# Decoder step on one core: memory tokens turned by VectorE in 32 x 32 blocks, with K/V weight rows loaded in the matching order

## The chip, the cores and the metric

The kernel runs on one core of a Trainium2 chip. The metric is the time of one execution on the device, in microseconds (us). Lower is better.

## The reference

One step of a decoder layer for 256 prompt tokens and 64 sample tokens (8 sequences of 8), 320 in all, with D = 2048, in float32. The parts that matter here:

```python
h = rms_norm(x, attn_norm_g);  z = h @ w_in       # u, v, glu_a, glu_b, q, gates
# three branches (spatial gating, conv module, cross-attention), gated, merged,
# @ w_o, then RMSNorm and a squared-ReLU MLP of 4*D, then a final RMSNorm
...
def mem_kv(mem, mem_norm_g, w_mem_kv):            # mem: 256 tokens x 2048
    kv = rms_norm(mem, mem_norm_g) @ w_mem_kv     # w_mem_kv: 2048 x 2048
    k, v = jnp.split(kv, 2, axis=-1)              # 1024 columns each, 4 heads of 256
```

K and V of the prompt's memory are outputs, and the prompt's cross-attention uses them.

## The kernel before, in words

All products run at float32 accuracy as three matmuls on two-part numbers: each operand is split into a high part (rounded to float32r) and a low part (the residue), and hi x hi, hi x lo and lo x hi are added in PSUM. ScalarE makes the high part of a weight tile (`split_to`, lines 252 and 278) and VectorE the low part (`residue_to`, recorded at line 44 as all VectorE work is).

The whole kernel is one list of 544 "halves". A half is 256 rows by 512 columns of some weight matrix, 512 KB, in two row blocks of 128 (k = 0, 1). Halves are grouped by 512 output columns; a group over 2048 rows has eight halves. In "T" halves the weights are the stationary operand and 320 tokens stream past (24 matmuls, lines 1341 to 1343). In "N" halves, those of `w_mem_kv`, the turned memory is stationary and 512 weight columns stream (twelve matmuls, lines 1371 to 1373). The order is: glu_b and glu_a (halves 0 to 31), q (32 to 47), kv (48 to 79, the N halves), the gate of branch C (80 to 111), u, v, and so on.

At the start of half i the loop asks for the weight load of half i+4 on SP's queue (`load_to`; three buffers `wraw`, so a load waits until VectorE is done with the one three before), then ScalarE's split of half i+2, then VectorE's residue of half i+1, and in the middle of the half VectorE's residue of half i+2. Everything else is a "side step", put by hand into the list `side[i]` of some half and issued between its matmuls (`spread` lays a list of steps over a range of halves, leaving out halves that end a group; `later` puts one step at one half).

The memory takes this way. `mem_load(0)` and `mem_load(1)` at halves 16 and 17 load 128 tokens per partition row (two token blocks by 1024 channels). Four `mem_sq_step`s in halves 22 to 31 add the squares of each token, which lie along one partition's row, on ScalarE. Sixteen `mem_tr_step`s in halves 32 to 47 turn one block of 128 channels each: two TensorE transposes into PSUM (line 748), then ScalarE's high part times the gain `mem_norm_g` (line 118), then VectorE's low part. `mh` and `ml` hold the turned memory, channel on the partition, token along the row; the root mean square of a token is multiplied in when K and V leave PSUM (`evac_kv`).

VectorE also computes the depthwise convolution, as 248 taps of two instructions each (`conv_step`), and these have no fixed place. `pace` adds taps to a half as long as the estimated VectorE time of the half (`V.spent`, by the rates of `PacedVector`: 0.08 us and 0.00105 us an element, a transpose 0.0023, copies 0.0006) stays under 0.75 of the half's 3.2 us (2.6 in N halves). Taps still left at half 184 are all issued there, ahead of the layer norm that needs them.

Of the kernel before, what the change touches and what calls it, by code (L numbers as in the profile page):

```python
# [10 lines left out]
F32R = mybir.dt.float32r  # L11
AF = mybir.ActivationFunctionType
ALU = mybir.AluOpType
AX = mybir.AxisListType

D = 2048
# [4 lines left out]
EPS = 1e-6  # L21
CONV_PACE = 0.75
WARM = 5
LO_HI, HI_LO, MEM_OFF = 40, 24, 8
QUARTER = (0, 1)


# [22 lines left out]
def decoder_step_kernel(  # L50
# [8 lines left out]
    nc = tc.nc  # L59
    V = PacedVector(nc.vector)  # L60
# [5 lines left out]
    def sb(shape, tag, dt=F32, bufs=1, name=None):  # L66
        counter[0] += 1
        return pool.tile(shape, dt, tag=tag, name=f"{name or tag}_{counter[0]}", bufs=bufs)
# [5 lines left out]
    def ps_misc(shape):  # L74
        counter[0] += 1
        return psum.tile(shape, F32, tag="misc", name=f"misc_{counter[0]}", bufs=2)
# [14 lines left out]
            for o in (0, 8 * NT + LO_HI)  # L91
        ]

    def mem_block(tag, name):
        flat = sb([128, 16 * 256 + MEM_OFF], tag, F32R, name=name)
        return flat[:, MEM_OFF:].rearrange("p (k t) -> p k t", t=256)

    def place():

# [10 lines left out]
    def f32(ap):  # L110
        return ap.bitcast(F32)
# [5 lines left out]
    def split_scaled(hi, lo, src, g):  # L117
        nc.scalar.activation(hi, src, AF.Copy, scale=g)
        V.scalar_tensor_tensor(
            out=lo, in0=src, scalar=g, in1=f32(hi), op0=ALU.mult, op1=ALU.subtract  # L120
        )
# [51 lines left out]
    def rstd_col(sums, scale, n=1, then=None, gap=1, between=()):  # L173
        c = sb([128, 3, 4], "rs", bufs=2)
        v, t, r = c[:, 0, :n], c[:, 1, :n], c[:, 2, :n]
        rstd_chain(v, r, lambda: t, sums, scale, then, gap, between)
        return r
# [48 lines left out]
    def pieces(j):  # L226
        return (slice(0, 1), slice(1, 2)) if j == 0 else (slice(0, 2),)

    def load_to(i):
        while issued[0] <= min(i, NH - 1):  # L230
            j = issued[0]
            g, h = halves[j]
            t = sb([128, 2, 512], "wraw", bufs=RAW_BUFS, name="wraw")
            r0 = (g["k0"] + 2 * h) * 128
            src = g["src"][r0:r0 + 256, g["n0"]:g["n0"] + 512].rearrange("(k p) n -> p k n", p=128)
            for ks in pieces(j):
                nc.sync.dma_start(t[:, ks], src[:, ks])
            raws[j] = t
            issued[0] += 1

# [21 lines left out]
    def split_alloc(j):  # L262
        hi = sb([128, 2, 512], "whi", F32R, bufs=3, name="whi")
        parts[j] = [hi, raws.pop(j)]

    def residue_alloc(j):
        parts[j].append(sb([128, 2, 512], "wlo", F32R, bufs=3, name="wlo"))
# [27 lines left out]
    def spread(lo, hi, steps):  # L295
        slots = [i for i in range(lo, hi) if not ends[i]] or [lo]
        for s, fn in enumerate(steps):
            side[slots[s * len(slots) // len(steps)]].append(fn)

    def later(at, fn):  # L300
        side[at].append(fn)

    S = {}


    def prologue():
        rest = sb([104, 128], "tr", bufs=3, name="vrows")
        S["rest"] = rest
        ag = sb([16, 128], "tr", bufs=3, name="agrows")
        nc.sync.dma_start(ag, attn_g[0].rearrange("(r c) -> r c", c=128))  # L310
        xn = sb([128, 2, D], "T1", name="xn")
        xs = sb([64, D], "T2", name="xs")
        xp_v = x_prompt[0].rearrange("(t p) d -> p t d", p=128)
        xs_v = x_sample.rearrange("b s d -> (b s) d")
        def x_load(c0, w):
            cs = slice(c0, c0 + w)
            nc.sync.dma_start(xn[:, :, cs], xp_v[:, :, cs])
            nc.sync.dma_start(xs[:, cs], xs_v[:, cs])

        S["x_load"] = x_load  # L320
        for j, (c0, w) in enumerate(((0, 256), (256, 256), (512, 512))):
            x_load(c0, w)
            load_to(j)

        S["ones"] = sb([128, 128], "ones")
        V.memset(S["ones"], 1.0 / 1024)
        wp = ps_misc([128, 512])
        for _ in range(WARM):
            nc.tensor.matmul(wp[:, :128], S["ones"], S["ones"], start=True, stop=True)
        warm = sb([128, 1], "warm")  # L330
        nc.scalar.activation(warm, S["ones"][:, 0:1], AF.Copy)
        S["xss"] = sb([128, 3, 4], "xss")
        V.memset(S["xss"], 1.0)
        ident = sb([128, 128], "ident")
        make_identity(nc, ident)
        S["ident"] = ident

        r0 = 0
        S["col"] = {"attn_g": 104}
        for name, src, n in (  # L340
            ("mlp_g", mlp_g, 16), ("mem_g", mem_g, 16), ("b_gate", b_gate, 48),
            ("conv_b", conv_b, 8), ("conv_ln_g", conv_ln_g, 8), ("conv_ln_b", conv_ln_b, 8),
        ):
            nc.gpsimd.dma_start(rest[r0:r0 + n, :], src[0].rearrange("(r c) -> r c", c=128))
            S["col"][name] = r0
            r0 += n
        vecs = sb([128, 120], "vecs")
        S["vecs"] = vecs
        vp = ps_misc([128, 512])
        nc.tensor.transpose(vp[:, :16], ag, ident[:16, :16])  # L350
        V.tensor_copy(vecs[:, 104:120], vp[:, :16])

        S["hh"] = sb([128, 16, NT], "HH", F32R, name="hh")
        S["hl"] = sb([128, 16, NT], "HL", F32R, name="hl")
        S["toks"] = [(xn[:, 0], 128, 0), (xn[:, 1], 128, 128), (xs, 64, 256)]
        split_alloc(0)
        residue_alloc(0)
        issued[1] = issued[2] = 1
        for k in range(2):
            x_in_step(k)  # L360
            split_part(0, k)
            residue_part(0, k)
        load_to(3)
        S["x_load"](1024, 512)

    def x_in_step(m):
        pt = ps_misc([128, 512])
        for a, p, c0 in S["toks"]:
            nc.tensor.transpose(  # L369
                pt[:, c0:c0 + p], a[:, 128 * m:128 * (m + 1)], S["ident"][:p, :p]  # L370
            )
        split(S["hh"][:, m], S["hl"][:, m], pt[:, :NT])
# [44 lines left out]
    def col(name, i):  # L417
        c = S["col"][name] + i
        return S["vecs"][:, c:c + 1]
# [293 lines left out]


    def mem_load(i):
        if i == 0:
            S["mem"] = [None, None]
            S["mss"] = sb([128, 2, 2], "mss")
        t = sb([128, 2, 1024], ("T7", "T4a")[i], name="mem")
        nc.sync.dma_start(  # L720
            t, mem_prompt[0, :, 1024 * i:1024 * (i + 1)].rearrange("(t p) d -> p t d", p=128)
        )
        S["mem"][i] = t

    def mem_sq_step(i, t):
        for c in range(2):
            d = sb([128, 512], "at", bufs=3)
            src = S["mem"][i][:, t, 512 * c:512 * (c + 1)]
            acc = sb([128, 1], "ss", bufs=3)
            nc.scalar.activation(d, src, AF.Square, accum_out=acc)  # L730
            tot = S["mss"][:, 0, t:t + 1]
            if i == 0 and c == 0:
                V.tensor_copy(tot, acc)
            else:
                V.tensor_tensor(out=tot, in0=tot, in1=acc, op=ALU.add)
        if i == 1 and t == 1:
            S["mrstd"] = sb([128, 2], "mrstd")
            r = rstd_col(
                S["mss"][:, 0], 1.0 / D, 2, lambda: V.tensor_copy(S["mrstd"], r)
            )  # L740

    def mem_tr_step(k):
        if k == 0:
            S["mh"] = mem_block("T1", "mh")
            S["ml"] = mem_block("T2", "ml")
        p = ps_misc([128, 2, 256])
        for t in range(2):
            nc.tensor.transpose(
                p[:, 0, 128 * t:128 * (t + 1)],
                S["mem"][k // 8][:, t, 128 * (k % 8):128 * (k % 8 + 1)], S["ident"],  # L750
            )
        split_scaled(S["mh"][:, k], S["ml"][:, k], p[:, 0], col("mem_g", k))

    def kT_step(n, t, kn):
        if n == 0 and t == 0:
# [460 lines left out]
    with tc.manual_schedule():  # L1216
# [17 lines left out]
        q0, kv0, u0, c0 = f[("q", 0)], f[("kv", 0)], f[("u", 0)], f[("gC", 0)]  # L1234
        v0, w0, a1, g0 = f[("v", 0)], f[("wC", 0)], f[("gA", 0)], f[("gB", 0)]
        later(16, lambda: mem_load(0))
        later(17, lambda: mem_load(1))
        spread(q0 - 10, q0, [lambda i=i, t=t: mem_sq_step(i, t) for i in range(2) for t in range(2)])
        spread(q0, q0 + 16, [lambda k=k: mem_tr_step(k) for k in range(16)])

        def attn_begin():
            hs = [attn_prompt_steps(h) for h in range(4)]
# [59 lines left out]
        for i, (g, h) in enumerate(halves):  # L1302
# [8 lines left out]
            hi, _, lo = parts.pop(i)  # L1311
            last = h == g["nk"] // 2 - 1
            if i == 0:
                for mi in range(4):
                    accs[mi] = ps_main([128, 512])
                for k in range(2):
                    for xs_, ws in ((0, hi), (1, hi), (0, lo)):
                        for mi in range(4):
# [3 lines left out]
                                stop=False,  # L1322
# [8 lines left out]
            elif g["kind"] == "T":  # L1331
                for mi in range(4):
                    if h == 0:
                        accs[mi] = ps_main([128, 512])
                    a = accs[mi][:, :NT]
                    c = 2 * (mi % 2) + mi // 2 if key[0] == "q" else mi
# [26 lines left out]
            else:  # L1363
                for t in range(2):
# [3 lines left out]
                    for k in range(2):  # L1368
                        kk = 2 * h + k
                        mh, ml = S["mh"][:, kk, ms], S["ml"][:, kk, ms]  # L1370
# [50 lines left out]
```

## Time and profile before

| what | value |
|---|---|
| time, median of 3 runs | 1978.63 us (1975.5 to 1981.38) |
| time of the profiled execution | 1981.95 us |
| its span in the profile | 1980.2 us |
| TensorE busy, share of the span | 1955.4 us, 99% |
| VectorE, ScalarE, GpSimd busy | 1184.9, 821.6 and 44.6 us |
| share of the chain that ended last: TensorE, DMA, VectorE | 94%, 2%, 2% |
| moved by DMA | 319.25 MB, 161 GB/s over the span |
| loads of `w_mem_kv`: count, size, median time from issue to landing | 32 of 512 KB, 4.1 us |
| loads of the memory | 2 of 1024 KB, 8.6 us |

How to read it: PE is TensorE's matmuls, PEld its weight loads, DVE is VectorE, ACT ScalarE, POOL GpSimd, SP the engine whose queue issues most loads. A line such as L748 is a line of the kernel. In a group's row stand the instruction, out<-in with the program's names, shapes, count, then busy time, mean nanoseconds of one, and the idle time before it with what ended it. Matmuls overlap, so their durations (0.3 us) are longer than the distance between two starts. In a table of stretches each row gives the stretch, its length, busy time and count for each engine, the granted TensorE clock, the busy share of the sixteen DMA engines, and GB/s.

### The profile page before, as it was taken

To read this page: it belongs to the slowest core of one execution; us is meant where nothing else is said; L and a number is where in the kernel's file an instruction comes from. 1 tells how busy PE (TensorE), PEld (TensorE's weight loads), DVE (VectorE), ACT (ScalarE), POOL (GpSimd) and SP (SyncE) were. 2 spreads that over 40 slices of the span, in tenths; PEclk is the share of its full clock that TensorE was granted. 3 is DMA by queue.
4 is the path that set the end of the run, shared out by engine and by line. 5 is a ranking of instruction groups with operands and counts; after the bars stand their busy time and mean duration, and the time that the engine had idled before them with its cause. 6 is when DMAs were issued, how large, how long until landed. Compare 5 with 4: busy or idle time off the path is not lost.

```text
span 1980.2 us, 32516 instructions
## 1 busy us (share of the span) xinstructions
PE 1955.4 (99%) x13316; PEld 1912.6 (97%) x13316; DVE 1184.9 (60%) x2079; ACT 821.6 (41%) x1185; POOL 44.6 (2%) x88
## 2 busy tenths in 40 slices
PE   9999999999999999999999999999999999999997
PEld 8999789898999999999999999999999999999997
DVE  4687786576788768655556554445434554455544
ACT  6465445445543445444444333333333333333333
POOL 0001000100100000000000000000000000000000
PEclk9999999999999999999999999999999999999998
DMA  6554864998644445454445445444445544455443
GB/s 213 184 150 150 211 220 110 228 206 217 185 157 144 149 140 160 139 167 153 149 160 171 147 141 170 150 150 145 154 160 152 151 143 162 153 156 146 149 155 107
DMA packets 189971, 319.25 MB, mean 161 GB/s; under 512 B 43761, under 2 KB 44489, under 8 KB 189686
## 3 DMA queue, kind: packets, MB, share of 16 engines
q1 hardware_dynamic: 184798, 302.56, 51.3%
q0 software_dynamic: 5024, 14.62, 2.9%
q8 instruction: 104, 1.70, 0.4%
q14 instruction: 45, 0.37, 0.1%
HBM read 311.48 MB, written 6.09 MB: 160 GB/s over the span
## 4 chain that ended last, share of the span: by engine, by line
PE 94%; DMA 2%; DVE 2%; ACT 1%; issue 0%; SPq 0%; DVEq 0%; ACTq 0%
PE acc L1341 29%; PE acc L1343 29%; PE acc L1342 29%; DMA wraw<-in_w_in_dram 2%; PE acc L1373 1%; PE acc L1372 1%; PE acc L1371 1%; DVE wlo L44 1%; DMA wraw<-in_w_mem_kv_dram 0%; PE misc L924 0%; PE misc L369 0%; PE misc L874 0%; PE acc L1319 0%; DVE dc L44 0%; PE misc L773 0%
## 5 line engine op out<-in xcount | busy, mean ns | idle before, releaser
L1341 PE MATMUL acc<-hh,whi 128*128 128x320 f32 x2424 | 756.2, 312 | 0.0
L1343 PE MATMUL acc<-hh,wlo 128*128 128x320 f32 x2424 | 748.7, 309 | 0.0
L1342 PE MATMUL acc<-hl,whi 128*128 128x320 f32 x2424 | 739.0, 305 | 0.0
L44 DVE TENSOR_TENSOR wlo<-wraw,whi 128x1024 fp32r<-128x1024 f32 x368 | 449.0, 1223 | 416.6 <-ACT whi L278 416.5
L278 ACT ACTIVATE whi<-wraw 128x1024 fp32r<-128x1024 f32 x368 | 389.5, 1058 | 690.6 <-PE acc L1342 571.8
L1341 PEld LDWEIGHTS acc<-hh,whi 128*128 128x128 f32 x2424 | 456.8, 188 | 8.4 <-issue 7.0
L1342 PEld LDWEIGHTS acc<-hl,whi 128*128 128x128 f32 x2424 | 456.6, 188 | 0.4
L1343 PEld LDWEIGHTS acc<-hh,wlo 128*128 128x128 f32 x2424 | 454.7, 188 | 0.0
L252 ACT ACTIVATE whi<-wraw,vecs 128x512 fp32r<-128x512 f32 x352 | 236.5, 720 | 278.2 <-PE acc L1342 184.2
L1341 PE MATMUL acc<-ah,whi 128*128 128x320 f32 x1024 | 315.8, 308 | 0.0
L1343 PE MATMUL acc<-ah,wlo 128*128 128x320 f32 x1024 | 315.5, 308 | 0.0
L1342 PE MATMUL acc<-al,whi 128*128 128x320 f32 x1024 | 311.4, 304 | 0.0
L44 DVE SCALAR_TENSOR_TENSOR wlo<-wraw,vecs,whi 128x512 fp32r<-128x512 f32 x352 | 248.6, 748 | 81.4 <-ACT whi L252 80.7
L1341 PEld LDWEIGHTS acc<-ah,whi 128*128 128x128 f32 x1024 | 192.5, 188 | 0.0
L1342 PEld LDWEIGHTS acc<-al,whi 128*128 128x128 f32 x1024 | 192.3, 188 | 0.0
L1343 PEld LDWEIGHTS acc<-ah,wlo 128*128 128x128 f32 x1024 | 191.5, 187 | 0.0
L44 DVE SCALAR_TENSOR_TENSOR dc<-cx,rstd,dc 128x256 f32<-128x256 f32 x480 | 153.2, 379 | 0.0
L1343 PE MATMUL acc<-moh,wlo 128*128 128x320 f32 x256 | 79.1, 309 | 0.0
L1341 PE MATMUL acc<-moh,whi 128*128 128x320 f32 x256 | 78.7, 308 | 0.0
L44 DVE TENSOR_TENSOR res<-res,acc 128x320 f32<-128x320 f32 x80 | 38.9, 486 | 66.5 <-PE acc L1343 66.4
L1342 PE MATMUL acc<-mol,whi 128*128 128x320 f32 x256 | 78.1, 305 | 0.0
L1072 ACT ACTIVATE ah<-tr 128x320 fp32r<-128x320 f32 x64 | 30.2, 472 | 66.9 <-DVE tr L44 66.9
(243 smaller groups left out, 1700.4 us busy)
## 6 DMA issues: line engine op xcount, KB each, us to landing
wraw<-in_w_in_dram SPq DMA_DIRECT2D x175, 512.0 KB, 4.4
wraw<-in_w_up_dram SPq DMA_DIRECT2D x128, 512.0 KB, 3.8
wraw<-in_w_down_dram SPq DMA_DIRECT2D x128, 512.0 KB, 3.7
wraw<-in_w_mem_kv_dram SPq DMA_DIRECT2D x32, 512.0 KB, 4.1
wraw<-in_w_o_dram SPq DMA_DIRECT2D x32, 512.0 KB, 3.7
cache<-in_cache_mem_k_dram SPq DMA_DIRECT2D x32, 256.0 KB, 7.7
cache<-in_cache_mem_v_dram POOLq DMA_DIRECT2D x32, 256.0 KB, 7.1
wraw<-in_w_c_out_dram SPq DMA_DIRECT2D x16, 512.0 KB, 4.0
```

The lines of the kernel that those rows point to most:

```text
L44: return fn(*args, **kw)
L252: nc.scalar.activation(hi, t, AF.Copy, scale=col("attn_g", 2 * h + k))
L278: nc.scalar.activation(parts[j][0], parts[j][1], AF.Copy)
L1072: nc.scalar.activation(out, in_, fn, **kw)
L1341: nc.tensor.matmul(a, hi[:, k, ms], xh, start=(kk == 0), stop=False)
L1342: nc.tensor.matmul(a, hi[:, k, ms], xl, start=False, stop=False)
L1343: nc.tensor.matmul(a, lo[:, k, ms], xh, start=False, stop=(last and k == 1))
L1371: nc.tensor.matmul(accs[t], mh, hi[:, k], start=(kk == 0), stop=False)
L1372: nc.tensor.matmul(accs[t], mh, lo[:, k], start=False, stop=False)
L1373: nc.tensor.matmul(accs[t], ml, hi[:, k], start=False, stop=(last and k == 1))
```

## The change

The memory is loaded in another layout. Tile i (of two) holds on partition 32q + r, at place g, 256 channels from 512q + 256i of token 32g + r. A 32 x 32 block transpose on VectorE, in place, then puts a channel on each partition and 256 tokens along the row, with no TensorE and no PSUM in it. Block k of the turned memory so holds channels 512q + 32k + j on partition 32q + j, where it held channels 128k + p. The rows of `w_mem_kv` are loaded in the same order: block k takes 32 rows from each quarter of the matrix, and each half's load is written as two loads of one block. The column of gains `mem_norm_g` is loaded in that order too. A token's squares now lie on four partitions, one for each quarter; one small matmul with a selection matrix (built from the identity) adds them over the quarters, and a mask picks the place of each token. The steps of halves 32 to 47 become one `mem_rstd_step` and sixteen `mem_turn_step`s.

```diff
@@ load_to
-            src = g["src"][r0:r0 + 256, g["n0"]:g["n0"] + 512].rearrange("(k p) n -> p k n", p=128)
-            for ks in pieces(j):
-                nc.sync.dma_start(t[:, ks], src[:, ks])
+            cols = slice(g["n0"], g["n0"] + 512)
+            if g["kind"] == "N":
+                src = g["src"][:, cols].rearrange("(q k i) n -> k q i n", q=4, i=32)
+                for k in range(2):
+                    nc.sync.dma_start(t[:, k], src[2 * h + k])
+            else:
+                src = g["src"][r0:r0 + 256, cols].rearrange("(k p) n -> p k n", p=128)
+                for ks in pieces(j):
+                    nc.sync.dma_start(t[:, ks], src[:, ks])
@@ prologue (rows of the small vectors)
-            nc.gpsimd.dma_start(rest[r0:r0 + n, :], src[0].rearrange("(r c) -> r c", c=128))
+            rows, dst = src[0].rearrange("(r c) -> r c", c=128), rest[r0:r0 + n, :]
+            if name == "mem_g":
+                rows = src[0].rearrange("(q k i) -> k q i", q=4, i=32)
+                dst = dst.rearrange("k (q i) -> k q i", i=32)
+            nc.gpsimd.dma_start(dst, rows)
@@ mem_load
-        t = sb([128, 2, 1024], ("T7", "T4a")[i], name="mem")
-        nc.sync.dma_start(
-            t, mem_prompt[0, :, 1024 * i:1024 * (i + 1)].rearrange("(t p) d -> p t d", p=128)
+        t = sb([128, 8, 256], ("T7", "T4a")[i], name="mem")
+        for q in range(4):
+            c0 = 512 * q + 256 * i
+            nc.sync.dma_start(
+                t[32 * q:32 * (q + 1)],
+                mem_prompt[0, :, c0:c0 + 256].rearrange("(g r) c -> r g c", r=32),
+            )
@@ squares: 16 of 256 channels in place of 8 of 512
+    def mem_sq_step(i, a):
+        for g in range(4 * a, 4 * a + 4):
+            d = sb([128, 512], "at", bufs=3)
+            nc.scalar.activation(
+                d[:, :256], S["mem"][i][:, g], AF.Square, accum_out=S["mss"][:, i, g:g + 1]
+            )
+    def mem_rstd_step():
+        mss, ident = S["mss"], S["ident"]
+        V.tensor_tensor(out=mss[:, 0], in0=mss[:, 0], in1=mss[:, 1], op=ALU.add)
+        sel = sb([128, 128], "at", bufs=3)
+        quarter = ident.rearrange("p (a r) -> p r a", a=4)
+        V.tensor_reduce(sel[:, 0:32], quarter, axis=AX.X, op=ALU.add)
+        for a in range(1, 4):
+            V.tensor_copy(sel[:, 32 * a:32 * (a + 1)], sel[:, 0:32])
+        p = ps_misc([128, 512])
+        nc.tensor.matmul(p[:, :8], sel, mss[:, 0], start=True, stop=True)
...
@@ turning
-        p = ps_misc([128, 2, 256])
-        for t in range(2):
-            nc.tensor.transpose(
-                p[:, 0, 128 * t:128 * (t + 1)],
-                S["mem"][k // 8][:, t, 128 * (k % 8):128 * (k % 8 + 1)], S["ident"],
-            )
-        split_scaled(S["mh"][:, k], S["ml"][:, k], p[:, 0], col("mem_g", k))
+        m = S["mem"][k // 8][:, :, 32 * (k % 8):32 * (k % 8 + 1)]
+        V.transpose(m, m)
+        hi, lo = (S[n][:, k].rearrange("p (g r) -> p g r", r=32) for n in ("mh", "ml"))
+        split_scaled(hi, lo, m, col("mem_g", k))
@@ order of steps
-        spread(q0, q0 + 16, [lambda k=k: mem_tr_step(k) for k in range(16)])
+        spread(q0, q0 + 16, [mem_rstd_step] + [lambda k=k: mem_turn_step(k) for k in range(16)])
```

The tiles `mh` and `ml` also start at new offsets inside their buffers (8 and 24 elements, where both had 8).

More of the change, by code (lines that the diff above doesn't have):

```diff
@@ L23 @@
 WARM = 5
-LO_HI, HI_LO, MEM_OFF = 40, 24, 8
+LO_HI, HI_LO = 40, 24
+MH_OFF, ML_OFF = 8, 24
 QUARTER = (0, 1)
@@ L92, in both, with mem_block @@
         ]
-    def mem_block(tag, name):
-        flat = sb([128, 16 * 256 + MEM_OFF], tag, F32R, name=name)
-        return flat[:, MEM_OFF:].rearrange("p (k t) -> p k t", t=256)
+    def mem_block(tag, name, off):
+        flat = sb([128, 16 * 256 + off], tag, F32R, name=name)
+        return flat[:, off:].rearrange("p (k t) -> p k t", t=256)
     def place():
@@ L717, in mem_load @@
             S["mem"] = [None, None]
-            S["mss"] = sb([128, 2, 2], "mss")
-        t = sb([128, 2, 1024], ("T7", "T4a")[i], name="mem")
-        nc.sync.dma_start(
-            t, mem_prompt[0, :, 1024 * i:1024 * (i + 1)].rearrange("(t p) d -> p t d", p=128)
-        )
[L723 to L739, printed above, removed]
-            )
@@ L742, in mem_tr_step @@
-    def mem_tr_step(k):
-        if k == 0:
-            S["mh"] = mem_block("T1", "mh")
-            S["ml"] = mem_block("T2", "ml")
-        p = ps_misc([128, 2, 256])
-        for t in range(2):
-            nc.tensor.transpose(
-                p[:, 0, 128 * t:128 * (t + 1)],
-                S["mem"][k // 8][:, t, 128 * (k % 8):128 * (k % 8 + 1)], S["ident"],
-            )
-        split_scaled(S["mh"][:, k], S["ml"][:, k], p[:, 0], col("mem_g", k))
+            S["mss"] = sb([128, 4, 8], "mss")
@@ new lines, in mem_load @@
+        t = sb([128, 8, 256], ("T7", "T4a")[i], name="mem")
[5 more added lines that the diff above has]
+            )
+        S["mem"][i] = t
+    def mem_sq_step(i, a):
[4 more added lines that the diff above has]
+            )
@@ new lines, in mem_rstd_step @@
+    def mem_rstd_step():
[8 more added lines that the diff above has]
+        nc.tensor.matmul(p[:, :8], sel, mss[:, 0], start=True, stop=True)
+        S["mrows"] = rows = sb([128, 4], "mrows")
+        V.tensor_reduce(
+            rows, ident.rearrange("p (a r) -> p a r", a=4), axis=AX.X, op=ALU.add
+        )
+        for t in range(2):
+            V.tensor_tensor(
+                out=mss[:, 2, 4 * t:4 * t + 4], in0=p[:, 4 * t:4 * t + 4], in1=rows, op=ALU.mult
+            )
+        tot = mss[:, 3, 0:2]
+        V.tensor_reduce(
+            tot, mss[:, 2].rearrange("p (t a) -> p t a", t=2), axis=AX.X, op=ALU.add
+        )
+        S["mrstd"] = sb([128, 2], "mrstd")
+        r = rstd_col(tot, 1.0 / D, 2, lambda: V.tensor_copy(S["mrstd"], r))
@@ L754, in kT_step, with mem_turn_step @@
+    def mem_turn_step(k):
+        if k == 0:
+            S["mh"] = mem_block("T1", "mh", MH_OFF)
+            S["ml"] = mem_block("T2", "ml", ML_OFF)
+        m = S["mem"][k // 8][:, :, 32 * (k % 8):32 * (k % 8 + 1)]
+        V.transpose(m, m)
+        hi, lo = (S[n][:, k].rearrange("p (g r) -> p g r", r=32) for n in ("mh", "ml"))
+        split_scaled(hi, lo, m, col("mem_g", k))
     def kT_step(n, t, kn):
@@ L1237, in decoder_step_kernel @@
         later(17, lambda: mem_load(1))
-        spread(q0 - 10, q0, [lambda i=i, t=t: mem_sq_step(i, t) for i in range(2) for t in range(2)])
-        spread(q0, q0 + 16, [lambda k=k: mem_tr_step(k) for k in range(16)])
+        spread(q0 - 10, q0, [lambda i=i, a=a: mem_sq_step(i, a) for i in range(2) for a in range(2)])
+        spread(q0, q0 + 16, [mem_rstd_step] + [lambda k=k: mem_turn_step(k) for k in range(16)])
         def attn_begin():
```

## The prediction

> **What bounds the kernel now.** I read the page first: busy shares, DMA queues, the chain that ended last.
>
> ```profile
> span 1980.2 us, 32516 instructions
> PE   1955.4 (99%) x13316; PEld 1912.6 (97%) x13316; DVE 1184.9 (60%) x2079; ACT 821.6 (41%) x1185; POOL 44.6 (2%) x88
> q1 hardware_dynamic: 184798, 302.56, 51.3%
> PE 94%; DMA 2%; DVE 2%; ACT 1%; issue 0%; SPq 0%; DVEq 0%; ACTq 0%
> ```
>
> TensorE is the bound: 94% of the chain, with the DMA engines half busy on average. An average says nothing of the one stage that this change touches, so the next view is busy time by stretches: two of the q projection (halves 32 to 47, where the memory is turned), then four of the K/V projection (halves 48 to 79, on the memory's own weights).
>
> ```profile
> 135.00:165.00 30.00, 30.00 (x212) 29.50 (x212) 23.12 (x56) 17.07 (x31) 4.87 (x10) 1.00 0.53 152
> 165.00:195.00 30.00, 30.00 (x211) 29.62 (x211) 23.63 (x53) 15.16 (x27) 3.82 (x8) 1.00 0.49 149
> 195.00:219.00 24.00, 24.00 (x111) 20.05 (x110) 20.51 (x40) 9.19 (x10) 0.39 (x1) 1.00 0.59 196
> 219.00:243.00 24.00, 23.79 (x108) 19.36 (x107) 16.29 (x34) 9.15 (x11) 0.73 (x2) 1.00 0.99 219
> 243.00:267.00 24.00, 23.15 (x106) 18.84 (x105) 19.68 (x39) 12.67 (x15) 1.62 (x3) 1.00 0.66 220
> 267.00:292.00 25.00, 25.00 (x120) 21.18 (x119) 21.75 (x47) 11.91 (x16) 1.62 (x3) 1.00 0.71 217
> ```
>
> Columns are PE, PEld, DVE, ACT, POOL, granted clock, DMA share, GB/s. In q, TensorE never rests and DMA is half used. In K/V a half has twelve matmuls in place of 24 for the same 512 KB, so loads run at 196 to 220 GB/s, and at 219 to 243 us all sixteen engines are full (0.99). The K/V stage is the one part of the kernel with little DMA to spare; its edges are the first and last matmul on the turned memory.
>
> ```profile
> L1371 PE MATMUL acc<-whi,mh x128: 388/394/477, 196.8 to 287.6; 128*128 128x512 f32 x128
> L1373 PE MATMUL acc<-whi,ml x128: 392/394/397, 197.3 to 288.1; 128*128 128x512 f32 x128
> L237 SPq DMA_DIRECT2D wraw<-in_w_mem_kv_dram x32: 367/368/1714, 182.9 to 274.3; - x32
> ```
>
> So it runs from 196.8 to 288.5 us (288.1 and one matmul); its loads are issued from 182.9.
>
> **The change, in q.** Sixteen pairs of transposes leave TensorE. Their price is read from the order of time around the first pair.
>
> ```profile
> 135.70 0.31 PE L1343 MATMUL acc<-hh,wlo 128*128 128x320 f32 x1
> 135.84 0.38 PE L748 MATMUL misc<-ident,mem 128*128 128x128 f32 x2
> 135.98 0.39 PE L1341 MATMUL acc<-hh,whi 128*128 128x320 f32 x1
> 136.21 0.31 PE L1342 MATMUL acc<-hl,whi 128*128 128x320 f32 x1
> 136.35 0.31 PE L1343 MATMUL acc<-hh,wlo 128*128 128x320 f32 x1
> ```
>
> Matmuls start 0.14 apart (136.21 to 136.35). From L1343 to the second matmul after it would be 0.29; it is 0.51. A pair costs 0.22, sixteen 3.5 us, all on the bound engine. Against it stands one matmul with the selection, which waits for VectorE: an add, a reduction of 128 by 128, three copies, all issued just ahead of it.
>
> ```profile
> L44 DVE COPY mss<-ss x2: 154/154/155, 102.3 to 112.8; 128x1 f32<-128x1 f32 x2
> L44 DVE TENSOR_REDUCE soft<-misc 128x1 f32<-128x256 f32 x8 | 3.4, 419 | 0.8 <-PE misc L874 0.8
> L44 DVE STREAM_TRANSPOSE cache<-cache 128x256 f32<-128x256 f32 x64 | 24.1, 419 | 0.2 <-issue 0.2
> L44 DVE SCALAR_TENSOR_TENSOR ml<-misc,vecs,mh 128x256 fp32r<-128x256 f32 x16 | 7.7, 481 | 11.9 <-ACT mh L118 11.9
> L44 DVE SCALAR_TENSOR_TENSOR dc<-cx,rstd,dc 128x256 f32<-128x256 f32 x240 | 114.8, 478 | 0.0
> L44 DVE SCALAR_TENSOR_TENSOR dc<-cx,rstd,dc 128x64 f32<-128x64 f32 x240 | 66.9, 279 | 0.0
> L730 ACT ACTIVATE at<-mem 128x512 f32<-128x512 f32 x8 | 4.9, 615 | 0.0
> ```
>
> Four small ones at 0.154 and a reduction between 0.154 and 0.419 make 0.8 to 1.0 us. Nothing on TensorE can pass the matmul in the queue, so it costs between nothing (VectorE early) and 1.6 (VectorE a residue late); I take 1.0, its own time with it. Net gain in q: 2.5 us.
>
> VectorE gets sixteen turns at 0.419, 6.7 us, and keeps the sixteen residues at 0.481, which go on waiting for ScalarE's copy. The planner charges each turn 0.67, so it puts off convolution taps: followed half by half through its rule (budget 2.4 per half, a tap 0.50) 14 taps move out of q. A tap is 0.478 + 0.279, so q loses 10.6 us of VectorE work for the 6.7: VectorE does not become the bound there. The put-off taps fill the next free budget, at halves 177 to 182 where the old list had run out, two halves ahead of the layer norm at 184: no cost. Sixteen squares of 256 in place of eight of 512 are bounded by the whole group again, 8 x 0.615 = 4.9 us of ScalarE and its reads over ten halves; a ScalarE that is 41% busy covers it. Eight loads for two of the memory: the six more issues, at 0.37 us as for a weight load below, stand in SP's queue ahead of the weight loads of halves 21 and 22, which are asked for four halves early; the first square comes five halves later. The permuted mem_g rows, sixteen of four pieces each, are the second of six small loads in POOL's queue at the very start, and the first reader of any of them stands at half 7. All hidden.
>
> **The change, in K/V.** Each 512 KB load becomes two of 256 KB whose source is 4 (q) by 32 (i) by 512, where it was 128 by 2 by 512. SP's second issue is 0.37 us a half (367 ns in the row of the K/V loads): hidden. What is not plainly hidden is how many DMA engines such a load is dealt to. The trace has one place with loads of other outer counts, at 36 us: the old conv state (120 rows, twice), conv_w (31 rows), and the state copied on (8 blocks).
>
> ```profile
> cwn<-in_conv_w_dram SPq DMA_DIRECT2D x1, 124.0 KB
> 43.40:43.60 0.20, 1.00 0.56 195
> 44.00:44.20 0.20, 1.00 0.50 174
> 50.60:50.80 0.20, 1.00 0.00 0
> 51.00:51.20 0.20, 1.00 0.08 31
> 51.20:51.40 0.20, 1.00 0.05 20
> 53.20:53.40 0.20, 1.00 0.08 31
> q1 hardware_dynamic: 35, 0.07, 6.0%
> 57.00:57.50 0.50, 0.50 (x6) 1.00 1.02 397
> 38.00:38.50 0.50, 0.50 (x5) 1.00 1.06 414
> ```
>
> The second number from the right is the share of sixteen engines. After those loads half of the engines work alone for a while (0.50 is eight), and from 50.8 to 53.4 a single one does (0.06), bringing in 35 late packets of a weight load at 25 GB/s (20 and 31 in turn), or 82 ns for each 2 KB row. When all sixteen stream it is the same rate: 397/16 = 25. So loads here are not always dealt to all sixteen, 8 blocks seem to go to eight engines and 31 rows to one, a load is as late as its slowest engine, and an engine gives 25 GB/s. A load with 4 outer blocks then goes to four engines; I take them to be the same four each time, for no load here is told apart from the one before it.
>
> The Trainium skill says so outright ("DMA: Bandwidth & Descriptors", section "Why a DMA increments its semaphore by 16 and not by 1"): the engines used are the largest number up to 16 that divides the slowest dimension of both sides, the lowest-numbered ones. By that rule 4 against 128 gives four engines and the sum below; by an even spread the sum is the first rival. The same page's 27 GiB/s per engine would make the stage's 168 us below 145.
>
> Sum: 64 loads of 128 rows over four engines are 2048 rows on each, x 82 ns = 168 us. The same four engines carry a sixteenth each of the first key cache tile and of the K and V outputs.
>
> ```profile
> 345.00:345.50 0.50, 0.50 (x6) 1.00 1.37 158
> L278 ACT ACTIVATE whi<-wraw 128x1024 fp32r<-128x1024 f32 x368 | 389.5, 1058 | 690.6 <-PE acc L1342 571.8 <-DMA wraw<-in_w_up_dram 24.8 <-issue 24.0
> L44 DVE TENSOR_TENSOR wlo<-wraw,whi 128x1024 fp32r<-128x1024 f32 x368 | 449.0, 1223 | 416.6 <-ACT whi L278 416.5
> 368.00:371.00 3.00, 0.00 (x0) 1.00 1.05 244
> 371.50:375.00 3.50, 3.50 (x15) 0.52 1.14 186
> ```
>
> In key loads an engine gives 158/16 = 9.9 GB/s: four quarters of 16 KB, 6.6 us. Eight outputs of 16 KB at 25 GB/s: 5.2 us. Together 180 us. The first K/V load is issued 2.5 us earlier, at 180.4, and moves about 1.2 later: 181.6 + 180 = 361.6. Then come whi 1.06, wlo 1.22 and the last half's twelve matmuls (the stage before: 91.7 us over 32 halves, at most 2.8): the stage ends at 366.7, not 288.5. That is +78 us, the q gain in it, since three load buffers keep two loads waiting in the queue and the engines never pause. TensorE then rests half of the time. The rows at 368 to 375 us show its granted clock at 0.52 after a rest of three us; at half clock a half takes 5.5 us, 176 for 32, which still lies inside the 180: no further term. After the stage all is as before, later by 78. Against the profiled execution's own 1981.95 us that makes 2060; the median of the runs is 3.3 lower, so I say 2057.
>
> Bounds: at 414/16 = 26 GB/s (the row at 38.0 us) with caches and outputs at no cost, 161 us, +59. At the mean of the page, 302.56 MB in 51.3% of sixteen engines' 1980 us, 18.6 GB/s, the 168 become 225: +135.
>
> **Rivals.** First, not slower: the load is dealt evenly over all sixteen, because four by 32 rows are 128 rows all the same. Or the four engines change from load to load, which comes to the same, since four loads of 128 rows then fill sixteen. For it: the packets keep their 2 KB, and nothing in this trace is a weight load with four outer blocks. Against: the single late engine and the half-used sixteen above. Then only q counts: -3.5 + 1.0 = -2.5, 1976. It decides from 16 engines down to about eight, where 200 GB/s still meet the stage's 196 to 220. Second, eight engines (a deal over both dimensions): 84 + 12 us of load in a stage of 92, with the key tile on top, some +12: 1990. Third, four engines at the page's mean rate, because four lanes share one path: +135, 2114. The trace's lone engine speaks against it. Within the first rival, VectorE could fall behind in q: its rows show 77% busy and the residues' wait of 11.9 us before; with fewer taps I give that nothing of its own.
>
> **How the numbers follow.** Forecast 0.78, even spread 0.16, eight engines 0.02, slow lanes 0.04. The forecast's own range is 2038 (+59) to 2105; the range given, 2030 to 2118, goes 8 below the lower bound for the steps I left at nothing, reaches to the slow lanes, and leaves out the even spread, the eight engines and a little of the tails, about 0.2. A change below 0.3% (5.9 us) can't be told from none here. The even spread's -2.5 lies inside that: same 0.13, faster 0.03 if the selection matmul is free and the K/V stage also gains; all else is slower, 0.84.
>
> **What would show it.** Right: no transposes in q, q about 2.5 us shorter; in K/V a DMA share near 0.25 to 0.3 at about 100 GB/s, K/V loads landing after 8 us or more where they took 4, ScalarE waiting for them, a stage of some 170 us, TensorE half busy with spells of half clock, and everything after 370 us as before, shifted. The selection step is right if TensorE waits about a microsecond for VectorE at half 32. Wrong: if K/V loads land in 4 us at shares of 0.6 and more, they use all engines and the time is near 1976; if the share is 0.25 but the rate well under 100 GB/s, the row price failed; if q is longer, VectorE's turns are on the path after all.

## The result: 2074.2 us, 4.8% slower, and the profile after

| | before | after |
|---|---|---|
| time, median | 1978.63 us (1975.5 to 1983.5, 5 runs) | 2074.23 us (2071.3 to 2077.1, 5 runs) |
| profiled execution, its span | 1981.95, 1980.2 us | 2077.12, 2075.4 us |
| ratio | | 1.0477, interval 1.0462 to 1.0493 |

From the page of the changed kernel, the lines that answer to those quoted of the kernel before:

```profile
span 2075.4 us, 32552 instructions
PE 1993.5 (96%) x13286; PEld 1926.0 (93%) x13286; DVE 1190.9 (57%) x2096; ACT 823.0 (40%) x1201; POOL 44.4 (2%) x88
q1 hardware_dynamic: 186174, 302.56, 48.6%
PE 84%; DMA 9%; DVE 3%; ACT 2%; issue 0%; SPq 0%; ACTq 0%; DVEq 0%
```

The same bytes are moved, but DMA has 9% of the chain where it had 2%. Where that sits is seen in the stretches of the K/V stage (same columns as before: PE, PEld, DVE, ACT, POOL, clock, DMA share, GB/s):

```profile
205.00:211.00 6.00, 3.41 (x13) 2.17 (x12) 1.95 (x2) 1.06 (x1) 0.00 (x0) 1.00 0.26 99
229.00:235.00 6.00, 5.42 (x18) 3.44 (x16) 2.41 (x5) 1.06 (x1) 0.00 (x0) 0.80 0.26 100
265.00:271.00 6.00, 5.24 (x12) 3.88 (x13) 3.08 (x6) 1.06 (x1) 0.00 (x0) 0.55 0.43 117
313.00:319.00 6.00, 4.00 (x17) 2.76 (x16) 2.42 (x6) 1.06 (x1) 0.00 (x0) 1.00 0.26 100
```

99 to 100 GB/s at a share of 0.26 is four of sixteen engines, nearly always busy (4/16 = 0.25), at 25 GB/s each. The 0.43 is a key cache tile beside it. In the rows of the tiles, and of the waits from 180 to 400 us (microseconds in total, times, the longest):

```profile
L1399 PE MATMUL acc<-whi,mh x128: 388/398/776, 201.8 to 379.4; 128*128 128x512 f32 x128
L1401 PE MATMUL acc<-whi,ml x128: 387/396/632, 202.3 to 379.8; 128*128 128x512 f32 x128
L240 SPq DMA_DIRECT2D wraw<-in_w_mem_kv_dram x64: 528/556/5604, 189.3 to 361.1; - x64
L285 ACT ACTIVATE whi<-wraw x32: 1056/1056/1062, 198.3 to 375.0; 128x1024 fp32r<-128x1024 f32 x32
```

```profile
ACT whi L285 <- DMA wraw<-in_w_mem_kv_dram: 117.1, 26, 6.2
DVE wlo L45 <- ACT whi L285: 105.1, 31, 4.9
```

The stage runs from 201.8 to 380.2 us (379.8 and one matmul): 178.4 us in place of 91.7. ScalarE waits 117 us for weights, VectorE behind it, TensorE behind both. In q, TensorE rests where it never did; the waits from 80 to 205 us:

```profile
PE misc L757 <- DVE at L45: 1.8, 1, 1.8
PE misc L517 <- ACT at L513: 1.5, 2, 1.3
PE acc L1369 <- ACT whi L259: 1.3, 1, 1.3
ACT mh L119 <- DVE mem L45: 10.2, 8, 2.2
```

L757 is the selection matmul, L517 a transpose of the outgoing conv state that waits for ScalarE's copy (L513), L1369 a weight that landed late. The last row is ScalarE: its high parts wait 10.2 us for VectorE's turns. Of the 95.2 us by which the span grew, the K/V stage has 86.7, its later start 5.0 (201.8 for 196.8), and the time after it 3.5 (2075.4 - 380.2 = 1695.2 for 1691.7).

### The profile page after: what moved, and what is told of

Read it like the earlier page. It is cut to its first block, busy times and chain, and to the rows that moved or that the text cites. A ratio compares the mean times of both kernels' runs of the same rounds, so it can differ in the third digit from the quotient of the medians.

```text
span 2075.4 us, 32552 instructions
## 1 busy us (share of the span) xinstructions
PE 1993.5 (96%) x13286; PEld 1926.0 (93%) x13286; DVE 1190.9 (57%) x2096; ACT 823.0 (40%) x1201; POOL 44.4 (2%) x88
## 4 chain that ended last, share of the span: by engine, by line
PE 84%; DMA 9%; DVE 3%; ACT 2%; issue 0%; SPq 0%; ACTq 0%; DVEq 0%
PE acc L1369 27%; PE acc L1371 27%; PE acc L1370 27%; DMA wraw<-in_w_mem_kv_dram 7%; DMA wraw<-in_w_in_dram 2%; DVE wlo L45 2%; ACT whi L285 1%; DVE dc L45 1%; ACT whi L259 0%; PE misc L952 0%; PE misc L380 0%; PE misc L902 0%; PE acc L1347 0%; PE misc L845 0%; PE misc L801 0%
## 5 line engine op out<-in xcount | busy, mean ns | idle before, releaser
L1369 PE MATMUL acc<-hh,whi 128*128 128x320 f32 x2424 | 756.2, 312 | 1.3 <-ACT whi L259 1.3
L1369 PEld LDWEIGHTS acc<-hh,whi 128*128 128x128 f32 x2424 | 457.8, 189 | 10.0 <-issue 7.0
L1369 PE MATMUL acc<-ah,whi 128*128 128x320 f32 x1024 | 315.9, 308 | 0.0
L1369 PEld LDWEIGHTS acc<-ah,whi 128*128 128x128 f32 x1024 | 192.5, 188 | 0.0
L1399 PE MATMUL acc<-whi,mh 128*128 128x512 f32 x128 | 61.6, 481 | 25.9 <-ACT whi L285 25.9
L1400 PE MATMUL acc<-wlo,mh 128*128 128x512 f32 x128 | 63.0, 492 | 18.2 <-DVE wlo L45 18.2
L1369 PE MATMUL acc<-moh,whi 128*128 128x320 f32 x256 | 78.7, 308 | 0.0
```

Source lines behind the costliest of these rows:

```text
L1369: nc.tensor.matmul(a, hi[:, k, ms], xh, start=(kk == 0), stop=False)
L1399: nc.tensor.matmul(accs[t], mh, hi[:, k], start=(kk == 0), stop=False)
L1400: nc.tensor.matmul(accs[t], mh, lo[:, k], start=False, stop=False)
```

## The experiments

**How many engines a load gets.** Theory: a source with 4 outer blocks is dealt to four engines. Rival: something else in the change (layout of the memory, turns, two loads in place of one) stretches the stage. The kernel before, with only its K/V loads written with 4, 8 and 16 outer blocks:

```diff
-            src = g["src"][r0:r0 + 256, ...].rearrange("(k p) n -> p k n", p=128)
-            for ks in pieces(j): ...
+                src = g["src"][:, cols].rearrange("(q k i) n -> k q i n", q=4, i=32)   # q=8, i=16; q=16, i=8
+                for k in range(2):
+                    nc.sync.dma_start(t[:, k], src[2 * h + k])
```

> The kernel before, with only its K/V weight loads written as in the change (4 outer blocks of 32 rows, two loads a half); the memory is turned as before, so K and V come out with their rows in the wrong order. Theory (a load is dealt to as many engines as its outer count allows, here four): the K/V stage is held at 98 to 101 GB/s as in the changed kernel, 64 x 32 rows x 82 ns = 168 us and some 12 us of other loads; the stage takes 172 to 180 us in place of 91.7, and the time is 80 to 88 us above before, 2060 to 2067 us. Rival (VectorE's turns or the new memory layout cost the time): within 5 us of before.

> As outer4, but with 8 outer blocks of 16 rows; K and V again in the wrong row order. Theory: eight engines, 198 GB/s, 84 us for the loads and 6 to 12 us for the rest: the stage is just held by its loads, 95 to 105 us, so 3 to 14 us above before. Rival that two loads a half or the scattered rows cost the time, whatever the outer count: the same as outer4.

> As outer4, with 16 outer blocks of 8 rows: the same number of loads, the same 2 KB rows, equally scattered; K and V in the wrong row order. Theory: sixteen engines, nothing lost, within 4 us of before. Rival that the number of loads or the scatter costs the time: the same as outer4, 80 us or more.

Measured: 2066.57 us (ratio 1.0437, 1.0418 to 1.0457), 1991.0 (1.0061, 1.0038 to 1.0084) and 1980.97 (0.9999, 0.999 to 1.0009), each inside what was expected. Stretches of the K/V stage from each, in that order:

```profile
215.00:225.00 10.00, 7.28 (x27) 5.07 (x26) 4.82 (x10) 2.12 (x2) 0.00 (x0) 0.93 0.27 101
```

```profile
205.00:215.00 10.00, 10.00 (x45) 8.20 (x44) 7.81 (x18) 4.01 (x4) 0.00 (x0) 1.00 0.53 189
235.00:245.00 10.00, 8.31 (x33) 5.62 (x31) 5.10 (x12) 2.79 (x3) 0.00 (x0) 1.00 0.68 174
```

```profile
205.00:215.00 10.00, 10.00 (x45) 8.22 (x44) 9.24 (x20) 3.95 (x4) 0.00 (x0) 1.00 0.72 201
```

Shares of 0.27, 0.53 and 0.72 at 101, 189 and 201 GB/s: the first two are what 4 and 8 busy engines of sixteen give (0.25 and 0.50), and the third is more than eight. In `outer4` TensorE rests (7.28 of 10); in `outer16` it does not, so the loads no longer hold the stage. `outer8` lies between: TensorE is full in the stretch at 205 us and rests in the one at 235 us, where key cache tiles come in beside the weights (a share of 0.68), and ScalarE waits 50.1 us in all for K/V weights. Its stage lasts 102 us (195.0 to 297.2). Nothing but the outer count differs between the three, so it, and it alone, makes the four engines. The Trainium skill ("DMA: Bandwidth & Descriptors", "Why a DMA increments its semaphore by 16 and not by 1") has the number of engines as the largest up to 16 that divides the outermost count of both sides; all three runs agree.

**The dealing undone in the changed kernel,** in two ways: `quarters` keeps the channel order and loads each quarter of a half by itself (32 outer rows, four issues a half); `affine` gives partition p of block (i, k) the channel 1024i + 8p + k, so that a half is again one load over 128 rows, and a turn takes every eighth channel of the tile (the memory's columns and the gains are loaded to match, which the cut below leaves out).

```diff
quarters:
+                src = g["src"][:, cols].rearrange("(q k i) n -> q i k n", q=4, i=32)
+                for q in range(4):
+                    nc.sync.dma_start(t[32 * q:32 * (q + 1)], src[q][:, 2 * h:2 * h + 2])
affine:
+                src = g["src"][1024 * (h // 4):1024 * (h // 4 + 1), cols].rearrange("(p k) n -> p k n", k=8)
+                nc.sync.dma_start(t, src[:, 2 * (h % 4):2 * (h % 4) + 2])
...
+        m = S["mem"][k // 8].rearrange("p g (j k) -> p k g j", k=8)[:, k % 8]
```

> The changed kernel with the K/V weights loaded by quarters: four loads a half, each 32 outer rows by 2 by 512 onto 32 partitions; all else as changed. Theory: sixteen engines again, the K/V stage back to 90 to 95 us, and left over is what the rest of the change costs: about 3 us lost while the memory loads, some 3.5 at the selection matmul with the slow clock after it, 3.5 won by the sixteen pairs of transposes. Time 1978 to 1985 us, up to 0.3% above before. Rival (the turning steps cost a good part of the 95 us): 2000 us or more.

> The changed kernel with another order of channels that keeps one K/V load a half with 128 outer rows: partition p of block (i, k) holds channel 1024i + 8p + k, so a half's weights are 128 rows apart by 8, two adjacent rows each, and VectorE turns every eighth channel. Theory: the K/V stage is 91 to 93 us as before; left are 3 us while the memory loads in 1 KB pieces and 3 to 4 around the selection matmul and the turns, less 3.5 for the transposes: 4 us above before (quarters minus the 6 that its four loads a half cost in K/V). Rival: turning every eighth channel is slow on VectorE (0.9 us and more in place of 0.44) and q is longer by 5 us or more.

Measured: `quarters` 1990.92 us (1.0054, 1.0035 to 1.0072), `affine` 1991.79 (1.0057, 1.0036 to 1.0077). Some 83 of the 95 us are gone with the dealing, so it is the cause of the bulk. But some 11 us stay in both, where I had expected at most 6 and 4: the first misses its forecast, and in the second the rival came true. In `quarters` the stage is 97.9 us long, six more than before, and the chain there shows four issues, one after another, ahead of a load (start, length, what):

```profile
218.59 0.31 SPq L240
...
218.94 0.42 SPq L240
...
219.41 0.42 SPq L240
...
219.88 6.76 DMA wraw<-in_w_mem_kv_dram
```

That the issues make the six us is argued. A rival was not tested: each of these loads goes to 32 partitions, and over the stage the engines are busier for a lower rate (a share of 0.84 for 196 GB/s, where the kernel before has 0.74 for 212).

In `affine` the stage is some 94 us, and most of the loss comes ahead of it: the stage starts at 203.5 us. The rows of its turns and residues, and its waits:

```profile
L45 DVE STREAM_TRANSPOSE mem<-mem x16: 664/738/784, 139.3 to 201.1; 128x256 f32<-128x256 f32 x16
L45 DVE SCALAR_TENSOR_TENSOR ml<-mem,gm,mh x16: 687/728/750, 140.8 to 202.7; 128x256 fp32r<-128x256 f32 x16
```

```profile
PE misc L515 <- ACT at L511: 5.9, 2, 3.4
PE misc L755 <- DVE at L45: 1.8, 1, 1.8
ACT mh L119 <- DVE mem L45: 22.6, 12, 3.1
```

Reading every eighth element makes a turn 0.738 us (0.438 in the changed kernel) and a residue 0.728 (0.485), and ScalarE waits for turns 22.6 us in place of 10.2. TensorE pays 5.9 us at the conv state's transposes, behind ScalarE. So a second cause is at work in q.

**Which part of q.** On `affine`, step by step: `spread` issues the memory's loads one a half (halves 11 to 14 and 16 to 19); `early` also builds the selection matrix eight halves ahead and puts its matmul into half 33; `ahead` also turns each block one step before the step that splits it.

```diff
spread:
-        later(16, lambda: mem_load(0)); later(17, lambda: mem_load(1))      # four issues each
+        for q in range(4):
+            later(11 + q, lambda q=q: mem_load(0, q)); later(16 + q, lambda q=q: mem_load(1, q))
early:
+        later(q0 - 8, mem_sel_step); later(q0 - 2, mem_add_step)            # matrix; sum of squares
+        later(q0 + 1, mem_sum_step); later(q0 + 2, mem_rstd_step)           # matmul; root
ahead:
     def mem_turn_step(k):
+        if k < 16:
+            m = mem_block_of(k)
+            V.transpose(m, m)
...
+        k -= 1
-        V.transpose(m, m)
-        split_scaled(hi, lo, m, ...)
+        split_scaled(hi, lo, mem_block_of(k), ...)
```

> affine with the eight memory loads spread over halves 11 to 14 and 16 to 19, one a half. Theory (at 82 to 101 us the 1 KB pieces fill the DMA engines at 205 GB/s and weight loads behind them land late): TensorE does not rest between 100 and 116 us, 2 to 3 us faster than affine. Rival (the pieces cost the same wherever they are loaded): no gain, the rest moves to another place.

> spread with the selection matrix built eight halves earlier, the add at half 30, the matmul at half 33 and what follows it at half 34. Theory (TensorE waited 1.84 us for VectorE's five operations, and may then run at half clock for some 3.4 us): 1.8 to 3.5 us faster than spread, no wait of TensorE for VectorE at the selection. Rival (VectorE is late there anyway, and TensorE next waits for a residue): under 0.5 us.

> early with each block turned one step ahead of its split, so that ScalarE's copy does not wait for the turn just ahead of it. Theory (in q, ScalarE waits some 10 us for turns and VectorE 13 to 16 us for ScalarE's copies, and TensorE is late by a part of it): 1 to 2 us faster than early and a little under before, 1976 to 1979. Rival (those waits lie inside the lead of two halves): no difference to early.

Measured: `spread` 1990.08 us (1.0048, 1.003 to 1.0066), not told apart from `affine`; `early` 1992.55 (1.0061, 1.0047 to 1.0076), nothing gained; `ahead` 1979.41 (0.9999, 0.9989 to 1.001), 13 us less than `early`. In the first two the rivals came true. In the third the theory had the cause and missed the size, 1 to 2 us for 13. The waits of `early`, then those of `ahead`:

```profile
PE misc L515 <- ACT at L511: 11.1, 2, 6.8
ACT mh L119 <- DVE mem L45: 19.7, 13, 2.8
```

```profile
PE misc L515 <- ACT at L511: 1.2, 2, 0.7
ACT mh L119 <- DVE mem L45: 1.3, 1, 1.3
```

In `early` the selection's wait of 1.8 us has left the list, and TensorE's wait for the conv-state copy has grown from 6.7 in `spread` to 11.1: the time moved on to the next late thing. What feeds it is the order within one step: turn on VectorE, copy on ScalarE, residue on VectorE. The copy stands at the head of ScalarE's queue until its turn is made, and the conv-state copies that TensorE needs stand behind it. With the turn one step earlier both waits go, though the turns are as slow as before (0.742). The edit also lays 17 steps over the same halves in place of 16, so copies shift a little against the conv-state steps; that shift alone was not tested.

**The same in the changed kernel, with four engines kept.** `turnahead` moves the turn alone; `asforecast` also takes the other two edits, so that q is as the forecast had it (diffs as above, on the contiguous blocks of the change).

> The changed kernel with one thing moved: VectorE turns block k+1 in the step in which ScalarE copies block k, so that no copy stands at the head of ScalarE's queue until its own turn is made. K/V loads stay at four outer blocks, memory loads and selection as changed. If the order turn, copy, residue within one step is what made q long, ScalarE's wait of 10.2 us for the turns goes below 2, the K/V stage starts 3 to 5 us before 201.8 us, and the whole shift reaches the end: 2069 to 2071 against 2074.2 (ratio to the kernel before 1.045 to 1.046). Rival, that q is long because of the late weight loads at 100 us and the selection matmul alone: no change, 2073 to 2075.

> The changed kernel with everything hidden that the forecast called hidden: turns one step ahead, memory loads one a half at halves 11 to 14 and 16 to 19, the selection matrix built eight halves early and its matmul a half later; the four-outer-block K/V loads stay. If those are all of the q stage's miss, K/V starts at 193 to 196 us (the forecast had 194.3 worked out as 196.8 less 2.5), lasts 178, and the time is 2063 to 2067: what is then left over 2057 is the longer stage (178 for 172) and the 3.5 us lost after it. Rival, that the start of the stage is set by the loads themselves (first issue, four engines), not by q: then the stage ends at 380 as before and the time stays at 2071 to 2075.

Measured: 2071.14 us (1.0445, 1.0421 to 1.047) and 2064.83 (1.0419, 1.0399 to 1.044). Both times come out as the theory had them, but the first gain, 3 us, does not stand clear of the scatter of its four runs (2064 to 2074) and is read from the trace: ScalarE's wait for turns is 0.5 us there, where the changed kernel has 10.2, and the stage starts earlier. Profiled executions differ by some 2 us in when the first phase ends, so the start of the K/V stage is counted here from the transposes of conv_w. The marks of the kernel before, the changed one and `asforecast`:

```profile
L444 PE MATMUL misc<-ident,cwn x8: 219/220/243, 50.1 to 50.5; 31*128 31x31 f32 x8
```

```profile
L455 PE MATMUL misc<-ident,cwn x8: 219/220/243, 50.1 to 50.5; 31*128 31x31 f32 x8
```

```profile
L455 PE MATMUL misc<-ident,cwn x8: 219/220/243, 48.0 to 48.5; 31*128 31x31 f32 x8
L1415 PE MATMUL acc<-whi,mh x128: 388/398/793, 192.2 to 370.4; 128*128 128x512 f32 x128
L1417 PE MATMUL acc<-whi,ml x128: 387/396/632, 192.7 to 370.9; 128*128 128x512 f32 x128
```

196.8 - 50.1 = 146.7 before, 151.7 in the changed kernel, 192.2 - 48.0 = 144.2 in `asforecast`: 2.5 us less than before. In `turnahead` it is 148.6 (196.4 - 47.8). This measure is steady: in `outer4`, `outer8`, `outer16` and `pieces` below, which all turn the memory on TensorE, it is 146.7 to 147.0. The stages of `turnahead` and `asforecast` last 177 and 179 us, so a change in q shifts the stage and does not shorten it.

**The memory's loads.** In the changed kernel TensorE rests near 100 us, which the kernel before does not. `pieces` is the kernel before with its two memory loads cut into eight of 1 KB pieces, over 128 rows as before.

```diff
-            t, mem_prompt[0, :, 1024 * i:1024 * (i + 1)].rearrange("(t p) d -> p t d", p=128)
+                t[:, :, 256 * q:256 * (q + 1)],
+                mem_prompt[0, :, c0:c0 + 256].rearrange("(t p) d -> p t d", p=128),
```

> The kernel before with the memory's two loads of 4 KB pieces cut into eight of 1 KB pieces, four issues after one another, in the old layout of 128 rows; all else as before. If the size of the pieces is what made the DMA engines slow at 82 to 101 us in the changed kernel (205 GB/s at full share), TensorE rests 1 to 2 us near 100 us here too and the time rises by 2 to 4 us, to 1982 to 1985. Rival, that the layout over 32 partitions did it: no rest, 1979 to 1982.

Measured: 1981.73 us (0.9996, 0.9983 to 1.0009): no change, and no rest of TensorE near 100 us. This speaks against the theory of the small pieces. The changed kernel, then `pieces`, in the stretches where the memory comes in:

```profile
80.00:92.00 12.00, 12.00 (x85) 12.00 (x84) 10.33 (x26) 3.56 (x6) 0.00 (x0) 1.00 0.81 179
92.00:100.00 8.00, 8.00 (x57) 8.00 (x56) 3.19 (x8) 1.34 (x2) 0.00 (x0) 1.00 1.11 253
100.00:105.00 5.00, 3.46 (x21) 2.72 (x20) 3.25 (x9) 4.00 (x7) 0.00 (x0) 1.00 0.44 130
```

```profile
80.00:92.00 12.00, 12.00 (x85) 12.00 (x84) 9.74 (x24) 4.02 (x6) 0.00 (x0) 1.00 0.94 299
92.00:100.00 8.00, 8.00 (x58) 8.00 (x57) 6.88 (x19) 4.23 (x7) 0.00 (x0) 1.00 0.66 208
```

Over 128 rows, 1 KB pieces run at 299 GB/s with the engines 94% busy; over 32 partitions they took a share of 1.11 for 253 and TensorE lost 1.5 us behind them. The same loads in `turnahead` cost 0.3 us (47.70 busy of 48 from 82 to 130 us, where the changed kernel has 46.20), so the size of this loss differs between profiles. It is 1.7 and 1.8 us in `quarters` and the changed kernel, whose conv_w mark lies at 50 us, and 0.3 and 0.4 us in `turnahead` and `affine`, whose mark lies at 48. The profile of `pieces` has its mark at 47.9, where little is lost in any case, so it settles less than its theory asked. Why loads over 32 partitions are slower stays open.

**A version against both.** `best` is `ahead` with the turn written to a tile of its own, contiguous, in a place that is free in q, so that copy and residue read in order.

```diff
-            V.transpose(m, m)
+            V.transpose(S["turned"][:, k % 8], mem_block_of(k))
```

> The kernel with turns one step ahead and K/V loads over 128 rows (1979.4), with each turn written to a contiguous tile, so that copy and residue read contiguously. Copies fall from about 0.8 to 0.5 us and residues from 0.73 to 0.49. If the order of the queue and not these durations was what counted, 1978 to 1980, no different. Rival, that the durations still count: K/V starts 2 to 3 us earlier and the time is 1976 to 1977, unless the stretch of full DMA at 340 to 450 us takes it back.

Measured: 1977.49 us (0.9983, 0.9971 to 0.9996), between the two forecasts. K/V starts 144.0 us after the mark (192.5 - 48.5), 2.7 less than before, and the gain, 3.6 us or 0.17%, is about the sum of the q stage; it is below the 0.3% that a few runs can tell, and shown only by eleven. Against `ahead` (193.3 - 48.2 = 145.1) the start is 1.1 us earlier, where the rival asked for 2 to 3: the order of the queue was most of it, the durations a little. With the 0.6 us of waits that are left at the conv state counted against it, taking TensorE's sixteen transposes out was worth 2.7 us.

## Why the prediction was right, and where its steps missed

- **Four engines at 25 GB/s** held, in the place and by the mechanism foreseen: 99 to 101 GB/s at a share of 0.26 and the stage twice as long. `outer4` shows it without the rest of the change, `outer16` shows it gone. Eight engines were priced at +12 and cost 10 to 12 (`outer8`: 9.8 us between the medians, 0.61% by the ratio). The late engine and the half-used sixteen at 36 us of the old trace were the right rows to read.
- **The size was 17 us short** (2057 for 2074). Against the predicted end of the stage at 366.7 us it came at 380.2, 13.5 later. 8.9 of it is the first K/V load, issued at 189.3 us and not 180.4 (the stage itself began 7.5 later than forecast, 201.8 for 194.3); 4.5 is the time from that issue to the last split (189.3 to 375.0, 185.7 us, where 180.4 to 361.6 was predicted). The price of a row held (32 x 524 KB at 99.5 GB/s are 168.6 us, put at 168), so by difference the key tile, the outputs and the first landing took 17 us where 13 was put. The tail behind the last split was 5.2 us, as predicted, though one of its terms is misread (91.7 us over 32 halves are 2.87, not "at most 2.8"). The 2105 at the top of the forecast's own range is added up from nothing that it shows. The other 3.5 came after the stage.
- **The step that failed is q,** put at -2.5 us. It was +5.0. "All hidden" did not hold of the memory's loads: TensorE rested 1.5 us at 100 to 105 us in that execution. The selection matmul, put at 1.0 with a bound of 1.6, waited 1.84 us: VectorE was in the residues of a weight tile (1.41 us) when the group ahead of the matmul came up, and the granted clock then fell to 0.67 and 0.50 for four microseconds:

```profile
142.00:144.00 2.00, 2.00 (x12) 2.00 (x11) 1.67 (x3) 0.50 (x2) 0.00 (x0) 0.67 0.58 224
144.00:146.00 2.00, 2.00 (x10) 2.00 (x9) 1.58 (x8) 1.32 (x3) 0.00 (x0) 0.50 0.68 188
```

- **The third loss in q was not in the prediction at all.** It asked whether VectorE has the time for the turns (it has) and not what waits behind them. A residue that "goes on waiting for ScalarE's copy" was noted; that the copy now waits for VectorE, which used to be TensorE's work, was not, nor that ScalarE's queue carries the conv-state copies on which TensorE depends. With the three mended, `asforecast` gets the predicted -2.5 from the start to the K/V stage, and 2064.8. That it is just this number is in part luck: the forecast had 3.5 won less 1.0 for the selection, and in `asforecast` TensorE does not wait for the selection at all. The list is not closed either. In the changed kernel TensorE's rests add up to 5.2 us (1.8 near 100 us, 1.84, and 1.5 at the conv state) and the slow clock to some 1.5 by my estimate (13 matmuls 0.27 apart in place of 0.145); less the 3.5 won this makes +3.2 of the +5.0.
- **"After the stage all is as before"** missed by 3.5 us. What stands behind the stage is a stretch in which the cache tiles keep all sixteen engines full; in the old trace it lies at 340 to 450 us, in the new one about a hundred later:

```profile
340.00:400.00 60.00, 56.29 (x409) 52.78 (x409) 37.82 (x84) 29.77 (x51) 6.31 (x12) 0.97 1.07 224
```

```profile
450.00:500.00 50.00, 46.34 (x335) 42.87 (x334) 31.47 (x71) 25.49 (x44) 6.41 (x13) 0.93 0.98 217
```

  It rests TensorE in both. That a different phase between the cache loads and the weights makes the 3.5 us is argued and was not tested. `asforecast` loses 3.4 there too (2066.4 - 371.3 = 1695.1), `best` 0.1 (1975.6 - 283.8 = 1691.8). But `outer4`, with the same long stage, loses only 0.6 (2063.8 - 371.5 = 1692.3), and `ahead`, whose stage is as short as before, 1.7 (1978.9 - 285.5 = 1693.4). With one profile of each, the 3.5 is not shown to belong to the change.
- **The half clock** in the stage stayed inside the loads' time, as predicted: granted clocks of 0.55 to 1.00 in the stretches above, while the engines' share never falls under 0.26 from 192 to 366 us. TensorE was not "half" busy, though: at the lower clock it is busy 127.2 of the stage's 178.4 us, 71%. The page gives no landing time for these loads, so the sign of "8 us or more" can't be read.

## What to carry to other kernels

When a load is rewritten, look at the outermost count of its access pattern before its bytes: with 4, 8 or 16 outer blocks the same 256 KB went to 4, 8 or 16 engines, and a layout whose rows are cut into four runs pays that on every load. When a step moves from one engine to another, do not ask only whether the new engine has time; follow each queue in order, and issue the producer one step ahead of the copy that waits for it. The gain from sixteen small transposes is real and small (2.7 us of the 3.5 they cost), so it can't carry any new wait.

## What the runs showed of the hardware that I had not expected

- A 32 x 32 turn of 128 x 256 on VectorE takes 0.438 us in order and 0.738 with a step of eight elements in source and place; writing in order and reading with the step is 0.694.

```profile
L45 DVE STREAM_TRANSPOSE mem<-mem x16: 435/438/441, 143.2 to 196.4; 128x256 f32<-128x256 f32 x16
```

```profile
L45 DVE STREAM_TRANSPOSE turned<-mem x16: 640/694/722, 135.5 to 183.0; 128x256 f32<-128x256 f32 x16
```

- The wait of 1.8 us on TensorE was followed by four microseconds of granted clock at 0.67 and 0.50, which the wait's own row does not show; `asforecast`, without that wait, keeps 1.00 through q (130 to 195 us).
- Loads of 1 KB pieces over 32 partitions gave 253 GB/s where the same pieces over 128 rows gave 299, with the engines fuller (a share of 1.11 for 0.94; weight loads run in both stretches).
